# Another engine opens and closes the block of hand-written synchronisation in a streaming kernel

One keyword in the kernel names the engine that opens and closes the block in which the kernel synchronises its engines by itself. The change names GpSimd in place of SyncE.

## The chip, the cores and the metric

The kernel runs on one core of a Trainium2 chip. The metric is the device time of one execution in microseconds (us). Several executions of each kernel were timed, and medians are quoted.

## The reference

```python
def setup_inputs():
    B, C, H, W = 8, 64, 256, 256
    return {"x": np.random.randn(B, C, H, W).astype(np.float32)}

def reference(x):
    ...   # pH = pW = 8
    x_r = x.reshape(B, C, oH, pH, oW, pW)
    pooled = x_r.max(axis=(3, 5))
    upsampled = np.repeat(np.repeat(pooled, pH, axis=2), pW, axis=3)
    return (x - upsampled).astype(np.float32)
```

Each 8 x 8 window loses its own maximum. 134 MB come in and 134 MB go out.

## The kernel before

Five slots form a ring in SBUF. SyncE issues the loads and waits for a slot's earlier store. VectorE takes the maxima (`tensor_reduce`) and subtracts them in place. ScalarE issues the stores. TensorE only passes on that a load has landed. GpSimd has no part in it. All of this stands in one block, `tile_critical`: inside it the framework adds no waits of its own, and the kernel's semaphores (counters with which one engine signals and on which another waits) do all the work.

```python
    with tc.tile_critical(no_gpsimd_drain=True):
        landed = [0] * SLOTS
        for i in range(len(sizes)):
            ...
            if landed[slot]:
                nc.sync.wait_ge(stored[slot], 16 * landed[slot])
            ...
                nc.sync.dma_start(out=sbuf(i, lo, R), in_=dram(x_rows, i)[:, part]).then_inc(...)
        ...
                nc.scalar.wait_ge(ready, done)
                nc.scalar.dma_start(out=dram(out_rows, i)[:, part], in_=sbuf(i, lo, R)).then_inc(...)
        ...
        nc.scalar.wait_ge(final, 16 * n_final)
        ...
        with nc.vector.Fori(0, TILES) as i:
            take(filled, 1)
            pool_and_subtract(...)
```

What the block costs shows in the built program. Its keeper, SyncE here, has an idle instruction (a NOP) ahead of the block, and every engine that works in it waits for that. After the block the keeper says that it is through. Each of the others then signs off with an instruction called DRAIN, and the keeper waits for these and ends with a second NOP. The program's last barrier, which GpSimd gathers, hangs on that NOP.

## Time and profile before

| | before |
|---|---|
| median of the first 3 executions, us | 626.66 (626.66 to 626.77) |
| span of the profile, us | 624.8 |
| VectorE busy | 90% |
| both DMA queues, share of 16 engines' span | 99.6% |
| DMA rate from 100 to 500 us | 433 GB/s |
| first load is issued at, us | 0.94 |
| SyncE's two NOPs, us | 0.7 and 624.0 |

The DMA engines are full, so the middle of the run is theirs. The change can only act at the two ends, and there a single sequencer instruction counts by what it releases and not by its own 13 ns. The profile's lines for this are shown in the prediction. In them DVE is VectorE, ACT ScalarE, POOL GpSimd, SP SyncE and PE or PEld TensorE; a q behind the name marks what the engine's instruction sequencer does by itself.

### The profile page before, as it was taken

What the parts mean: (1) busy time and instruction counts of PE and PEld (TensorE: products, weight loads), DVE (VectorE), ACT (ScalarE), POOL (GpSimd) and SP (SyncE); (2) the same over time, 40 slices, a digit from 0 to 9 for tenths busy, and PEclk for the clock granted to TensorE, in tenths of its full rate; (3) what the DMA queues carried; (4) which work ended last, traced back from release to release, by engine and by line L of the source; (5) the groups of instructions that cost most, each with busy time, mean ns of one, the idle gap of its engine ahead of it and who ended that gap; (6) DMA issues with size and microseconds to landing.
All of it is one profiled execution on the core that took longest, in us unless ns stands there. A gap on an engine that the chain in (4) does not pass through costs nothing. (4 is left out here: it accounts for less than half of the span.)

```text
span 624.8 us, 557 instructions
## 1 busy us (share of the span) xinstructions
DVE 561.1 (90%) x157; POOL 0.2 (0%) x4
## 2 busy tenths in 40 slices
DVE  4899999999989889898898898898898898988992
POOL 0000000000000000000000000000000000000000
DMA  9999999999999999999999999999999999999998
GB/s 366 406 457 441 420 420 461 420 420 461 420 420 461 420 420 461 420 420 461 420 420 461 420 420 461 420 420 461 420 420 461 420 420 459 422 422 442 450 422 352
DMA packets 8064, 268.44 MB, mean 430 GB/s; under 512 B 896, under 2 KB 896, under 8 KB 896
## 3 DMA queue, kind: packets, MB, share of 16 engines
q1 hardware_dynamic: 3888, 134.22, 49.9%
q10 hardware_dynamic: 4176, 134.22, 49.7%
HBM read 134.22 MB, written 134.22 MB: 430 GB/s over the span
## 5 line engine op out<-in xcount | busy, mean ns | idle before, releaser
L81 DVE TENSOR_REDUCE tops<-ring (+2 forms) x29 | 277.4, 9566 | 47.9 <-DVEq L75 39.6
L96 DVE TENSOR_TENSOR ring<-ring,tops (+1 forms) x128 | 284.4, 2285 | 3.9 <-DVEq L75 3.7
L165 POOL MEMSET const-bfloat16-1.0<- 128x1 bf16 x1 | 0.1, 102 | 0.0
L165 POOL MEMSET const-uint8-127<- 128x1 uint8 x1 | 0.1, 102 | 0.0
L165 POOL MEMSET const-float32-0.0<- 128x1 f32 x1 | 0.1, 99 | 0.2 <-issue 0.2
L165 POOL MEMSET const-float32-1.0<- 128x1 f32 x1 | 0.1, 99 | 0.0
## 6 DMA issues: line engine op xcount, KB each, us to landing
ring<-in_x_dram SPq DMA_DIRECT2D x24, 5120.0 KB, 57.6
out_dram<-ring ACTq DMA_DIRECT2D x24, 5120.0 KB, 40.7
out_dram<-ring ACTq DMA_DIRECT2D x3, 2048.0 KB, 20.9
ring<-in_x_dram SPq DMA_DIRECT2D x2, 2048.0 KB, 9.6
ring<-in_x_dram SPq DMA_DIRECT2D x1, 4096.0 KB, 55.1
out_dram<-ring ACTq DMA_DIRECT2D x2, 1024.0 KB, 11.8
```

Of the source, the lines that this page charges most:

```text
L81: nc.vector.tensor_reduce(out=maxs if R > 1 else maxs[:, 0], in_=(wins.rearrange("p r ph ow pw -> p r ow ph pw") if R > 1 else wins[:, 0]. ...
L96: sub = nc.vector.tensor_tensor(out=wins[:, r], in0=wins[:, r], in1=maxs[:, r].unsqueeze(1).unsqueeze(3).to_broadcast([P, pH, oW, pW]), op ...
L165: nc = _bacc.Bacc("TRN2", target_bir_lowering=False, num_devices=1)
```

## The change

The intent, as far as it can be read from the change: SyncE, which issues the loads, should not have to keep the block as well; GpSimd, which has nothing to do, can.

```diff
-    with tc.tile_critical(no_gpsimd_drain=True):
+    with tc.tile_critical(sync_engine=nc.gpsimd.engine, no_gpsimd_drain=True):
```

## The prediction

> **What bounds the kernel now.** I read the page's first two parts first (busy shares and the 40 slices), because they tell whether an engine or the transfers set the pace.
>
> ```profile
> DVE 561.1 (90%) x157; POOL 0.2 (0%) x4
> ...
> DMA  9999999999999999999999999999999999999998
> ...
> q1 hardware_dynamic: 3888, 134.22, 49.9%
> q10 hardware_dynamic: 4176, 134.22, 49.7%
> ```
>
> VectorE works 90% of the span and GpSimd next to nothing, but the DMA row is full in all but the last slice, and the two queues (loads on q1, stores on q10) together took 99.6% of what 16 DMA engines have in the span. So the 268 MB that go in and out are the bound. VectorE is the second one, and the groups and the waits say how far behind it is:
>
> ```profile
> L81 DVE TENSOR_REDUCE tops<-ring (+2 forms) x29 | 277.4, 9566 | 47.9 <-DVEq L75 39.6
> L96 DVE TENSOR_TENSOR ring<-ring,tops (+1 forms) x128 | 284.4, 2285 | 3.9 <-DVEq L75 3.7
> ```
>
> The reduce sits idle 47.9 us in all, 39.6 of it waiting at the helper of line 75, which waits for a landed load. Those are 19 waits, so about 2.1 us for each slot of five rows. VectorE is ahead of the data, and a few tens of ns more or less on its side vanish there.
>
> The change concerns the two ends of the block, so I cut the span into stretches. Columns: stretch, length, DVE busy, POOL busy, granted clock, DMA share, GB/s.
>
> ```profile
> 0.00:8.00 8.00, 0.00 (x0) 0.20 (x4) 1.00 0.78 295
> ...
> 100.00:500.00 400.00, 366.51 (x102) 0.00 (x0) 1.00 1.00 433
> ...
> 613.00:625.00 12.00, 0.00 (x0) 0.00 (x0) 1.00 0.79 336
> ```
>
> The middle runs at 433 GB/s. Only the first and last stretch are not full: there the DMA waits for the first issue, or the program waits for the last store. Whatever the change does to the time, it must do there, so I looked at who issues first, and at who waited last. First the timeline of the first 20 us, then SyncE's own waits:
>
> ```profile
> 0.33 0.10 POOL L165 MEMSET const-uint8-127<- 128x1 uint8 x1
> 0.94 2.90 SPq L113 DMA_DIRECT2D ring<-in_x_dram  x6
> 8.36 4.42 DVE L81 TENSOR_REDUCE tops<-ring 128x64 f32<-128x4096 f32 x1 [8.36 <-DMA ring<-in_x_dram]
> ```
>
> ```profile
> SPq L113 <- DMA out_dram<-ring: 528.4, 21, 51.3
> SPq L104 <- DVEq L104: 73.3, 1, 73.3
> SPq L104 <- ACTq L104: 10.8, 1, 10.8
> ```
>
> The four memsets of GpSimd are its whole work; the first load goes out at 0.94 us. At line 113 SyncE waits for stores, which is the ring being full. At line 104, the line that the change edits, it waits 73.3 us for VectorE and then 10.8 us for ScalarE, whose last store is in flight. Both waits are for work that has to end anyway. Line 104 itself is this short list over the whole run:
>
> ```profile
> L104 SPq EVENT_SEMAPHORE  x3: 17/17/28, 539.6 to 613.1; - x3
> L104 SPq NOP  x2: 13/13/13, 0.7 to 624.0; - x2
> L104 SPq DRAIN  x1: 57/57/57, 539.6 to 539.6; - x1
> L104 ACTq DRAIN  x1: 8/8/8, 623.9 to 623.9; - x1
> ```
>
> Two NOPs of SyncE open (0.7) and close (624.0) the block; everything else of it lies at 539.6 to 613.1, before the last store is even done.
>
> **What the Trainium skill says.** "Perfetto Trace Analysis", section "Sequencer-only Instruction (DRAIN, etc)": the window shown for such an instruction starts only when its wait is met, and the time in which its semaphore update spreads is not shown. So the 13 ns of a NOP are not its price; the price is from its start to the start of what it releases. The trace agrees: the opening NOP starts at 0.714 and is over at 0.727, but ScalarE's branch that waits for it starts at 0.750, 36 ns after the NOP's start. "Trainium Kernel Development and Optimization", section "Key Constraints": transfers of all issuing queues share the same 16 DMA engines. The trace agrees, with 49.9% and 49.7% of them. "DMA: Bandwidth & Descriptors", section "Specifications", gives a fabric ceiling of 435 GB/s and about 358 GB/s for one core's HBM. The trace runs at 433 in the middle, so it agrees with the first and not with the second. At 435, 268.44 MB need 617.1 us (an estimate, from that page's figure), which leaves 624.8 - 617.1 = 7.7 us for both ends together.
>
> **The change, part by part.** The start times to three decimals here and below are the trace's records of single instructions, which the views round to 0.1. The diff names GpSimd as the engine that opens and closes the block. No load, store, reduce or subtract moves: line 113 stays on SyncE, line 130 on ScalarE. I expect the opening NOP, the event that says that the block's own engine is through, the waits for the other engines' drains and the closing NOP to go over to GpSimd.
>
> *The opening.* Before: GpSimd releases the program's first barrier at 0.607; SyncE passes it at 0.649, does its NOP at 0.714, its branch at 0.784 and the first load at 0.937. The branch starts 70 ns after the NOP, where ScalarE's starts 36 ns after it, because on SyncE the NOP stands in its own way. After: GpSimd comes to its next instruction 81 ns after its release (its next one before was a DRAIN at 0.688), so the NOP falls at about 0.688. It is seen 36 ns later, at 0.724. SyncE, without a NOP of its own, could be at its branch at 0.649 + 0.065 = 0.714 and so takes it at 0.724 instead of 0.784. The first load is then out at 0.724 + (0.937 - 0.784) = 0.877. Sum: **0.06 us earlier**, and all of the DMA stream shifts with it, since every later transfer hangs on an earlier one.
>
> *The middle.* GpSimd has an empty body and says at once, not at 539.6, that it is through. The others' drains stand behind their own work in their own streams, so none of them can go ahead of it. Nothing is gained or lost: 0.
>
> *The closing.* Before: ScalarE passes the wait for the last stores at 623.765, drains at 623.920, SyncE's closing NOP follows at 623.954, then two drains of SyncE at 624.028 and 624.091, then GpSimd gathers the end barrier at 624.124. After: ScalarE's drain releases GpSimd's NOP, again 34 ns later. From there two strands run. SyncE's first drain waits for the NOP (36 ns), its second follows 63 ns later and GpSimd sees it 33 ns after that: 132 ns after the NOP. GpSimd itself has a drain and the gathering event left, at 79 ns from start to start (taken from its own drain at 624.586 and event at 624.665): 158 ns. The longer counts: 623.954 + 0.158 = 624.112, against 624.124. That is 0.01 us earlier, if ScalarE's drain is the last thing in GpSimd's list of waits. Were it waited for ahead of two others, it would be 2 x 79 = 0.16 us later. I can't see the order before the program is built, and choose +0.03 between the two, nearer to the order that SyncE has now (VectorE, then TensorE, then ScalarE).
>
> *Sum:* -0.06 + 0.03 = -0.03 us on 626.66, so **626.6**. This is some 1/200 of a per cent.
>
> **The rivals.**
>
> *GpSimd is the slow hand.* It does four memsets and a drain at the start (memsets until 0.435, drain until 0.485), and if its NOP had to wait for something behind these, or its sequencer took longer for each of some five waits, each would cost about 0.08 us: up to 0.4 us, so 627.0 to 627.1. Against it speaks that GpSimd releases the very first barrier, so it is ahead of all the others at the opening, and that its waits, apart from the one for ScalarE, will be met at 613 at the latest, 10.8 us ahead.
>
> *The stream is rearranged.* If loads start at another moment relative to stores, the 16 engines could mix the two queues differently, and a slot could come free later. VectorE's 2.1 us of slack for a slot would hide some of it, but the bound is the DMA and a hole in it counts. For it: the rate is not even, slices lie between 406 and 461 GB/s. Against: loads, reduces and stores all hang on one another, and all would shift by the same 0.06 us; and three executions before lie within 0.11 us. Were it so, I would expect under 1 us either way: 625.7 to 627.6.
>
> *SyncE freed, loads earlier.* The change may be meant so: SyncE is the load issuer and no longer has to keep the block. But its three events and its drain at line 104 lie after its last load (539.185), and the NOP ahead of its first one is worth the 0.06 us that I have counted. It would make 626.6, not less.
>
> **Range and chances.** The mechanism moves tenths of a us at most: from -0.1 to +0.5 with everything on one side. I add the scatter of the executions (0.11) and some for a different interleaving or chip: **626.1 to 627.1**. A change over 2% would take 12.5 us, that is over 150 of GpSimd's steps of 79 ns, or the loss of half a slot's worth of transfers. I see no way to it and give 0.01 to each side, 0.98 to within 2%.
>
> **What would show it.** Line 104 should list GpSimd's sequencer with two NOPs, and SyncE with none; the opening NOP near 0.69, the first load at 0.87 to 0.89 rather than 0.94. VectorE's first reduce should start about 0.06 us before 8.36. The slices of the DMA row, 433 GB/s in the middle, and VectorE's 561 us should be the same. From ScalarE's last drain to the gathering event of the end barrier there should be 0.19 to 0.36 us, where it is 0.20 now. I am wrong if the first load comes later than 0.94, if the stretch from 100 to 500 us moves by more than 1 GB/s, or if the tail after the last store grows by over 0.5 us.

## The result and the profile after

| | before | after |
|---|---|---|
| median of 6 executions each, us | 626.71 (626.65 to 626.79) | 626.69 (626.59 to 626.75) |
| span of the profile, us | 624.8 | 625.0 |

The ratio is 0.9999, with a 95% interval from 0.9987 to 1.0012: the same. A ratio here is the mean time of one kernel's fast runs over that of the other's of the same rounds, so it is not quite the ratio of the medians.

The page after, its busy shares, its 40 slices and its queues:

```profile
DVE 561.1 (90%) x157; POOL 0.2 (0%) x4
...
DMA  9999999999999999999999999999999999999998
...
q1 hardware_dynamic: 3888, 134.22, 49.9%
q10 hardware_dynamic: 4176, 134.22, 49.7%
```

All of these equal those before. The groups of VectorE, again from the page:

```profile
L81 DVE TENSOR_REDUCE tops<-ring (+2 forms) x29 | 277.4, 9566 | 48.0 <-DVEq L75 39.8
L96 DVE TENSOR_TENSOR ring<-ring,tops (+1 forms) x128 | 284.4, 2285 | 3.9 <-DVEq L75 3.7
```

The durations have not moved by a ns, and the wait for loads has grown from 39.6 to 39.8 us over the whole run, which is nothing. The stretches (stretch, length, DVE busy, POOL busy, clock, DMA share, GB/s):

```profile
0.00:8.00 8.00, 0.00 (x0) 0.20 (x4) 1.00 0.78 295
...
100.00:500.00 400.00, 366.65 (x102) 0.00 (x0) 1.00 1.00 434
...
613.00:625.00 12.00, 0.00 (x0) 0.00 (x0) 1.00 0.81 343
```

The middle runs at 434 GB/s, against 433; when both kernels ran once more (below), both had 433. The edit itself shows in two places: the timeline at the start, and the instructions of line 104 (engine, operation, count, durations in ns, first and last start in us).

```profile
0.88 2.88 SPq L113 DMA_DIRECT2D ring<-in_x_dram  x6
8.22 4.42 DVE L81 TENSOR_REDUCE tops<-ring 128x64 f32<-128x4096 f32 x1 [8.22 <-DMA ring<-in_x_dram]
```

```profile
L104 POOLq EVENT_SEMAPHORE  x3: 17/43/10856, 0.8 to 613.2; - x3
L104 POOLq NOP  x2: 13/13/13, 0.7 to 624.1; - x2
L104 SPq DRAIN  x1: 123/123/123, 539.6 to 539.6; - x1
...
L104 ACTq DRAIN  x1: 8/8/8, 624.0 to 624.0; - x1
```

The NOPs are GpSimd's now (POOLq), and the first load goes out at 0.88 instead of 0.94 us. Is SyncE free of the closing? Its own waits say no:

```profile
SPq L113 <- DMA out_dram<-ring: 528.6, 21, 51.5
SPq L176 <- DVEq L104: 73.3, 1, 73.3
SPq L176 <- ACTq L104: 10.9, 1, 10.9
```

The waits of 73.3 and some 10.9 us for VectorE and ScalarE are still there. They have only moved from line 104, the block, to line 176, the program's end, where SyncE must wait for all engines in any case. GpSimd waits for the same two beside it: the 10856 ns above is its wait for ScalarE.

The views round starts to 0.1 us, so both ends were laid out from the trace's records of single instructions. All times are us from the span's start:

```
opening                              before   after
GpSimd releases the first barrier     0.607   0.608
the keeper's NOP                      0.714   0.689
SyncE's branch into the block         0.784   0.728
first load                            0.937   0.881

closing, from ScalarE's last drain   before   after
ScalarE's drain (623.920 / 623.966)   0       0
the keeper's closing NOP              0.034   0.091
SyncE's first drain at the end        0.108   0.130
SyncE's second drain                  0.171   0.190
GpSimd gathers the last barrier       0.204   0.254
the program's last instruction ends   0.927   0.987
```

The opening became 0.056 us shorter and the closing 0.050 us longer up to the gathering event. From there to the end GpSimd's own instructions take another 0.010 us more, so the whole closing costs 0.060 us. The second pair of profiles below has the same: -0.053 us for the opening, and 0.059 us for the closing up to the end.

### The profile page after: what moved, and what is told of

The parts are those of the page before. It is cut to its first block, busy times and chain, and to the rows that moved or that the text cites. A ratio compares the mean times of both kernels' runs of the same rounds, so it can differ in the third digit from the quotient of the medians.

```text
span 625.0 us, 559 instructions
## 1 busy us (share of the span) xinstructions
DVE 561.1 (90%) x157; POOL 0.2 (0%) x4
## 5 line engine op out<-in xcount | busy, mean ns | idle before, releaser
L81 DVE TENSOR_REDUCE tops<-ring (+2 forms) x29 | 277.4, 9566 | 48.0 <-DVEq L75 39.8
```

Of the source, the lines that this page charges most:

```text
L81: nc.vector.tensor_reduce(out=maxs if R > 1 else maxs[:, 0], in_=(wins.rearrange("p r ph ow pw -> p r ow ph pw") if R > 1 else wins[:, 0]. ...
```

## The experiments

Eight kernels ran, the first four on one chip and the other four on another. All gave correct results. Beside the first four the kernel before had a median of 626.72 us (9 executions), beside the other four 626.70 (9 executions, the one at 628.64 among them).

Two theories were tested against the result. **A**: both ends are wholly exposed, all between them is moved bodily, and the two small changes cancel. **B**: the stream of transfers doesn't keep a shift, or scatters by as much as the change. Two more concern the hand: **C**, GpSimd is the slow one, and **D**, it is enough to save the hop between two engines.

### The kernel before, once more

No edit. It tells how far apart two executions of one program lie.

> The kernel before, unchanged, as a control of how far two executions of one program lie apart. Theory A (the two ends move by hundredths of a us, and what lies between is moved bodily): 626.7 us, first load at 0.93 to 0.94 us, and the starts of the later loads within 0.02 us of those of the first profile of this kernel. Theory B (the stream of transfers does not keep a shift; its own scatter is as large as the change): 626.6 to 626.8 us, the first six loads within 0.02 us of the earlier profile, but the later loads and reduces off by up to 0.15 us in both directions, although nothing was changed.

Measured: 626.63 us (626.62 to 626.67). The first six loads start within 0.01 us of those of the first profile. Here B's second half (the scatter) is right: with no edit at all the first reduce starts 0.13 us earlier, the third 0.07 us later, others up to 0.18 us earlier, and the last four within 0.01 us. So a difference of 0.1 us between two single profiles says nothing about the change.

### The changed kernel, once more

No edit to the changed kernel, on the same chip as the run above.

> The changed kernel, unchanged. Both theories: 626.7 us, the first load at 0.88 us, 0.05 to 0.06 earlier than in the kernel before, and 0.25 us from ScalarE's last drain to GpSimd's gathering event, against 0.20. Theory A: the loads after the first six again lie at the same distance from those of the kernel before as in the first pair of profiles (some 0.13 us later, then 0.05 later). Theory B: they lie elsewhere, with another sign in places.

Measured: 626.60 us (626.59 to 626.69). The first loads of the run above and of this one:

```profile
0.93 2.88 SPq L113 DMA_DIRECT2D ring<-in_x_dram  x6
```

```profile
0.88 2.90 SPq L113 DMA_DIRECT2D ring<-in_x_dram  x6
```

From ScalarE's drain to the gathering event it took 0.253 us, against 0.203 in the run above. So the closing repeats to 1 ns in both kernels, and the first load (0.934 and 0.881) to 3 ns. In the first pair of profiles the 7th to 14th loads were 0.12 to 0.14 us later after the change, which looked as if the earlier start had been lost. In this pair they are 0.04 to 0.05 us earlier, nearly like the first six (0.05 to 0.06), and the last ones 0.10 to 0.12 us earlier. The two profiles of the changed kernel alone differ by 0.10 to 0.12 us at the 7th to 14th load. The 0.13 us of the first pair was scatter.

### A late opening

```diff
     with tc.tile_critical(sync_engine=nc.gpsimd.engine, no_gpsimd_drain=True):
+        for _ in range(30):
+            nc.sync.sem_inc(spare, 1)
```

(and a semaphore `spare`, here and in the next run.)

> The changed kernel with 30 increments of a spare semaphore on SyncE ahead of its first load, at 65 to 78 ns each some 2.0 to 2.3 us. Theory A (the opening is wholly exposed, as the prediction has it): the first load at 2.9 to 3.2 us and the time longer by the same amount, 628.7 to 629.0 us. Theory B (the stream takes a shift up, because stores fill what loads leave): the first load as late as that, but the time longer by less than half of it, under 627.8 us.

Measured: 628.64 us (628.55 to 628.72), 2.04 more than the changed kernel in the same rounds. In the timeline of this kernel the first load is here:

```profile
2.68 2.38 SPq L116 DMA_DIRECT2D ring<-in_x_dram  x5
```

That is 1.80 us later, 60 ns for each of the 30 steps and so a little less than was expected. The delay is still there at the end: VectorE's last reduce starts 1.8 to 2.0 us later than in the two profiles of the changed kernel. The remaining 0.2 us between load and time is no larger than the scatter of single instructions. B's first half falls: a delay of 1.8 us is carried through 620 us of transfers (between 1.63 and 1.84 us of it at each load), and nothing in the stream makes up for it. That the 0.056 us of the change are carried too is concluded from this; in the times they are below the scatter.

### A late closing

```diff
         nc.scalar.wait_ge(final, 16 * n_final)
+        nc.gpsimd.wait_ge(final, 16 * n_final)
+        for _ in range(26):
+            nc.gpsimd.sem_inc(spare, 1)
```

> The changed kernel with GpSimd waiting for the last stores in the block and then doing 26 increments of a spare semaphore, at 79 ns each 2.05 us, before it says that it is through. Both theories: the closing hangs on GpSimd alone there, nothing lies beside it, so the time is 2.0 to 2.3 us longer, 628.7 to 629.0 us, with loads and stores as before. If it were less than 1 us longer, something else than the block's closing would end the program.

Measured: 628.82 us (628.72 to 628.84, and the one execution at 631.95), 2.22 more than the changed kernel. The added line and the block's line in this trace:

```profile
L138 POOLq EVENT_SEMAPHORE  x26: 17/17/17, 623.7 to 625.7; - x26
```

```profile
L105 POOLq NOP  x3: 13/13/13, 0.7 to 626.1; - x3
...
L105 ACTq DRAIN  x1: 8/8/8, 625.8 to 625.8; - x1
```

From the first increment (623.705) to the event that says that GpSimd is through (625.744) are 26 steps of 78 ns. Only then do the others drain, ScalarE at 625.8. The path from ScalarE's wait for the last store to the gathering event is 2.16 us longer than in the changed kernel. Each GpSimd step after the last store is on the path, at its full 78 ns.

### Ten small blocks by SyncE

```diff
+    for _ in range(10):
+        with tc.tile_critical(no_gpsimd_drain=True):
+            for engine in (nc.sync, nc.scalar, nc.tensor, nc.vector):
+                engine.nop(nofuse=True)
+
     with tc.tile_critical(no_gpsimd_drain=True):
```

> The kernel before with ten small blocks ahead of its block, each with one idle instruction on SyncE, ScalarE, TensorE and VectorE, all opened and closed by SyncE. It measures an opening and a closing with no transfers beside them. SyncE has about eight or nine sequencer steps in each, at 65 to 77 ns, so 0.5 to 0.7 us a block, and the first load at 6 to 8 us. Theory A (both engines do this at about the same price): the ten blocks by GpSimd are within 1 us of these. Theory C (GpSimd is the slow hand, 0.4 us more a block): those are 4 us longer.

Measured: 635.56 us (635.47 to 635.70), first load at 8.331, just past the 6 to 8 us expected. Undisturbed, a block takes 0.692 us from opening NOP to opening NOP; the last but one took 1.08.

### Ten small blocks by GpSimd

The same ten blocks on the changed kernel, with `sync_engine=nc.gpsimd.engine`.

> The changed kernel with the same ten small blocks, all opened and closed by GpSimd. Theory A: the first load within 1 us of that of the run with ten blocks by SyncE, and the time apart by just as much. Theory C: first load and time some 4 us later. If it is earlier than with SyncE, the opening's gain of 0.06 us outweighs the closing's loss of 0.05.

Measured: 634.63 us (634.52 to 634.86), first load at 7.439, and 0.65 to 0.69 us for a block. The instructions of the line of the ten blocks, first in the run by SyncE and then in this one:

```profile
L105 SPq EVENT_SEMAPHORE  x30: 17/17/28, 0.9 to 7.8; - x30
L105 SPq NOP  x20: 13/13/18, 0.7 to 7.9; - x20
...
L105 SPq DRAIN  x10: 7/7/7, 1.0 to 7.7; - x10
```

```profile
L105 POOLq EVENT_SEMAPHORE  x30: 17/17/133, 0.8 to 7.0; - x30
L105 POOLq NOP  x20: 13/13/13, 0.7 to 7.1; - x20
L105 SPq DRAIN  x10: 7/7/7, 0.9 to 6.8; - x10
```

C falls: nothing like 0.4 us a block is lost by GpSimd. Its single step is longer (from a block's closing NOP to the next one's opening NOP 92 to 95 ns, where SyncE's shortest are 66 to 67), but its whole block is up to 0.04 us shorter. Part of the 0.93 us between the two runs isn't the blocks': in the run by SyncE one block took 0.39 us more than the others, the first load's issue took 1.0 instead of 0.37 us, and ScalarE's drain came 0.42 us after its last wait instead of 0.16. The longer programs fetch instructions while they run: the records of instruction transfers have three packets of 8 KB after the span's start in the run by SyncE, at 7.7, 52.0 and 633.3 us, four in the run by GpSimd, the first at 38.4, and none in the kernel before. That these caused the delays is a guess from the times. Both runs are also longer by 1.4 to 1.5 us than their first load is late. The traces tell where, though not why: in the run by SyncE the second load is 8.02 us later than without the ten blocks and VectorE's last reduce 8.57, in the run by GpSimd 6.57 and 7.41, so the lateness grew in the stream; and in the run by GpSimd the end after the gathering event took 1.23 us instead of 0.73. So what is read here is the length of undisturbed blocks, not the time as a whole.

### ScalarE opens and closes

```diff
-    with tc.tile_critical(sync_engine=nc.gpsimd.engine, no_gpsimd_drain=True):
+    with tc.tile_critical(sync_engine=nc.scalar.engine, no_gpsimd_drain=True):
```

> ScalarE opens and closes the block. Its NOP at the opening should come at about 0.72, SyncE's branch at 0.76 and the first load at 0.91, between GpSimd's 0.88 and SyncE's 0.94. At the closing ScalarE is the last with work, so it says only after its wait for the last stores, at 623.8, that it is through, and its event, its drain, two waits and the closing NOP stand one behind another, at 65 to 80 ns each, after that. Theory A (what counts is how many steps come after the last store): 0.5 us or so from ScalarE's wait to the gathering event becomes 0.6 to 0.7, where it is 0.36 with SyncE and 0.41 with GpSimd; 626.8 to 627.0 us. Theory D (it is enough to save the hop between engines): shorter than with SyncE, 626.5 to 626.6 us.

Measured: 626.89 us (626.84 to 626.93), 0.19 more than the kernel before. The first load goes out at 0.919, between the other two. The instructions of line 104 of this kernel:

```profile
L104 ACTq EVENT_SEMAPHORE  x3: 17/17/38, 623.9 to 624.2; - x3
L104 ACTq NOP  x2: 14/16/18, 0.7 to 624.2; - x2
L104 SPq DRAIN  x1: 7/7/7, 624.0 to 624.0; - x1
L104 DVEq DRAIN  x1: 10/10/10, 624.0 to 624.0; - x1
```

All of the closing lies behind the last store: ScalarE can say only at 623.9 that it is through, and SyncE and VectorE, which drained at 539.6 and 610.7 before, do so at 624.0. From ScalarE's wait to the gathering event are 0.584 us, against 0.359 (SyncE) and 0.410 (GpSimd). With the 0.02 us won at the opening that makes 0.21, and 0.19 was measured. D falls: here a hop between engines was saved and the time grew. What fits all three keepers is the length of the chain after the last store.

### GpSimd is through late

```diff
         nc.scalar.wait_ge(final, 16 * n_final)
+        nc.gpsimd.wait_ge(ready, done)
```

> The changed kernel with GpSimd waiting in the block for VectorE's last subtract (at 613 us) before it says that it is through; in the changed kernel it says so at 0.77 us. Theory A (the closing is hidden behind the last store, 10.8 us, save for what hangs on ScalarE's drain): the drains of SyncE and TensorE move to 613 us and the time stays at 626.6 to 626.75 us. Theory C (a late GpSimd costs): longer by 0.3 us or more.

Measured: 626.78 us, just above A's range, in two pairs (626.61 and 626.64, 626.92 and 626.93). The profile, which is of one of the upper pair, has SyncE's drain at 613.4, so the edit did what it should:

```profile
L104 SPq DRAIN  x1: 7/7/7, 613.4 to 613.4; - x1
...
L104 ACTq DRAIN  x1: 8/8/8, 624.1 to 624.1; - x1
```

From ScalarE's drain to the gathering event it is 0.254 us, as in the changed kernel. The last reduce came 0.23 us later than in the first profile of the kernel before, but the loads were later by 0.14 to 0.21 us from the 13th on, at about 200 us, before GpSimd's late word can act on anything. The two lower executions are level with the changed kernel. So no cost of a late GpSimd shows; why two executions were 0.3 us longer stays open, and executions of the kernel before reached 627.0 and, in these very rounds, 628.64 too.

## Why the prediction was right

**The total.** Predicted 626.6 us, 626.1 to 627.1; measured 626.69, and 626.60 in the second rounds. The predicted change of -0.03 us can't be told from 0 by times: six executions of one kernel lie 0.14 to 0.16 us apart. What confirms the account is the ends in the trace, not the total: with every term of its sum under 0.2 us, a range of 1 us around no change was easy to hit.

**The opening** came out as worked out: the NOP at 0.689 (predicted 0.688), SyncE's branch at 0.728 (0.724), the first load at 0.881 (0.877), 0.056 us earlier instead of 0.06. The run with the late opening showed that a shift of 1.8 us is carried to the end, with 0.2 us of scatter.

**The middle** cost nothing, as predicted, and the run in which GpSimd is through only at 613 us fits that.

**The closing** was mis-sized by 0.02 to 0.03 us: +0.050 up to the gathering event, +0.060 up to the end, where the prediction chose +0.03 between two orders of the waits. That was a choice and no sum, and that it came near is in part luck. (Its worse order is 0.15 us above the time before by its own numbers, -0.01 + 0.16, and not 0.16.) The order was nearly the favourable one, but the step "ScalarE's drain releases GpSimd's NOP, again 34 ns later" was not right. In the program as built ScalarE is waited for by an instruction of its own, together with SyncE, and the NOP comes after it: 0.091 us instead of 0.034. The rest, from the NOP to the gathering event, is 0.163 us, against 0.158 predicted. Here GpSimd's own strand set the time, as the prediction had it; SyncE's second drain was over before. The 0.010 us after the gathering event were not in the prediction. The sum is -0.056 + 0.060 = +0.004 us, where -0.03 was predicted.

**The rivals.** The slow hand fell at the size that it named, up to 0.4 us, with the ten small blocks; what GpSimd costs at the closing is the 0.060 us above. The rearranged stream as a consequence of the change has nothing for it that repeats: the loads that came 0.13 us later in the first pair of profiles came 0.04 us earlier in the second. Two pairs can't exclude an effect below the scatter, and the scatter is there: single instructions of one program lie up to 0.27 us apart from execution to execution. The sign named for VectorE's first reduce, "about 0.06 us before 8.36", was a bad one for that reason: it came 0.14 us earlier after the change, and 0.13 earlier in the kernel before when run again. The third, SyncE freed, was right to expect nothing beyond the opening; SyncE even keeps two waits at the program's end.

An opening by GpSimd with a closing by SyncE would, as an estimate from these numbers, add up to -0.056 us. That is 0.01% and below what times can show, and the one keyword can't express it, so it was not built.

## What to carry to other kernels

In a kernel like this one, whose DMA engines are full from end to end, look before the first transfer and after the last one for what it does to move a duty from one engine to another. Lay out those two chains instruction by instruction, from start to start, and count the steps on them; most were worth 0.06 to 0.09 us here. Of the three engines tried, the one that finishes last, ScalarE, was the worst to close the block (0.584 us from its last wait to the gathering event, against 0.359 and 0.410). And before reading a difference of 0.1 us from two profiles, profile the unchanged kernel twice.

## What the Trainium skill lacked or had wrong

- "DMA: Bandwidth & Descriptors", section "Specifications", gives some 358 GB/s as the limit of HBM for one core, without a condition. Here reads and writes together held 433 to 434 GB/s for 400 us, close to the 435 that the same table gives for the fabric; the lower figure doesn't bound this mix of half loads and half stores by one core. The condition stands further down on that page, in section "Measured (HBM→SBUF, 128 partitions, SWDGE, issued from GpSimd)": about 358 GB/s each is what two cores get that stream from the same HBM domain. Every program here ran on one core.
- "Perfetto Trace Analysis", section "Sequencer-only Instruction (DRAIN, etc)", says that the spread of a semaphore update isn't shown, but gives no number. From the start of an opening NOP to the start of the first other engine's waiting branch were 35 to 41 ns, with SyncE, GpSimd or ScalarE as the keeper; the other engines' branches started up to 124 ns after it. The skill does have numbers for things near it, on the pages "Runtime: NRT & Kernel Launch" (a hop of the runtime's own barrier) and "Advanced Engine Details and Errata" (reading a semaphore), but none for this.
- The same section has no price of a step from start to start. The runs show 57 to 60 ns for most of 30 increments in a row on SyncE, 64 to 67 ns for most of SyncE's steps from NOP to NOP or from wait to wait, 78 ns for 26 increments in a row on GpSimd, and 92 to 95 ns for GpSimd from NOP to NOP. The least between two waits inside a block were 48 ns on SyncE and 60 on GpSimd.
- No page tells what it costs to open and close such a block: 0.69 us by SyncE and 0.65 to 0.69 us by GpSimd, with one idle instruction each on SyncE, ScalarE, TensorE and VectorE in it and nothing beside it.
